# One ring of four PSUM banks instead of two rings of two, from the state space stage on, in a two-block network kernel

## The chip, the cores and the metric

The kernel runs on 1 core of one Trainium2 chip, one launch from inputs to output. The time is the device time of that core in microseconds (us). All arithmetic of the reference is in float32. Where the text says median, it is the median over separate executions; the profile is of one further execution.

## The reference, cut to what matters

The reference is two blocks, `x = first_block(...)` and then `second_block(x, ...)`, on 256 tokens of width 1024. The first block (attention with an index, latent attention, cross attention, mixture of experts) is not touched. The second has two layers, and a second stream of 256 context tokens (`ctx`) beside `x`:

```python
def second_block(x, c, ctx, ...):
    for i in range(2):
        h_lat, h_ctx = modulated rmsnorm of x and of ctx
        if i == 0:  o_ctx, o_lat = ssd_mixer(h_ctx, h_lat, ...)     # state space, 8 groups of 4 heads
        else:       o_ctx, o_lat = attn_mixer(h_ctx, h_lat, ...)
        x = x + g1l * o_lat
        x = x + g2l * moe_ec(...)                                   # 16 experts choose their tokens
        if i == 0:  ctx = ctx + g1c * o_ctx;  ctx = ctx + g2c * moe_ec(...)
    return rmsnorm(x, final_norm_w)

# inside ssd_mixer, per group and chunk of 128 tokens:
    seg    = exp(where(tri, acum[..., :, None] - acum[..., None, :], -inf))
    cb     = einsum('bclgn,bcsgn->bcgls', Cc, Bc)
    y_diag = einsum('bcgrls,bcsgrp->bclgrp', cb[:, :, :, None] * seg, xdt)
    y_off  = einsum('bclgn,bcgrpn,bcgrl->bclgrp', Cc, h_prev, exp(acum))
    out    = rmsnorm((y + D_skip * x) * silu(z), norm_w) @ out_w
```

## The kernel before

The program is written against a tile framework. Tiles are taken from pools; a pool's tag with `bufs=n` is a ring of n buffers, and the framework makes the (n+1)th tile of a tag wait until the first has been read for the last time. The framework's scheduler then sets the order of each engine's instructions from the program order and its own model of when buffers come free (`schedule_with_timeline_sim=True` at the end of the listing). So a change of a ring's size changes the order in which instructions stand on the engines, and each engine then works its list strictly in that order. DMAs to and from DRAM are nearly all issued by SyncE (SP), in such a list too.

PSUM has 8 banks of 128 x 512 floats. `ps(tag)` (L93 to L95) takes one bank from a tag's ring; `psum(**bufs)` (L98) opens a set of rings. `run` (L2078) opens the set `four` (L2083) once for everything from the state space stage up to the end of layer 0's experts, and again for layer 1's experts. Between them the attention stage has its own set (`L=1, M=1, t=2, b=2`). The four tags of `four`:

- "p" (2 banks): projections (L1302 to L1304, `mm3`, three matmuls for each product of split floats), the modulation vectors (L1235), half of `ssd_out`, an expert's accumulators.
- "y" (2 banks): the outputs of a group (`yps`, L1576), the other half of `ssd_out`, accumulators.
- "t" (2 banks): the transposes (L1280, L1532, L1537, and in the experts' part L1721, L1750, L1761, L1842, L1861), and the product of the states with C (L1599), which DVE reads at L1600.
- "b" (2 banks): all other small products: `cb` (L1552), `seg` (L1563 and L1566), state sums (L1588), decays (L1594), the norm (L1656), the routing products (L1764, L1785), and the products that put the experts' outputs back in the tokens' places (L1873).

**State space stage** (about 438 to 1020 us). First the normed rows are transposed (`to_features_mod`, L1280): PE transposes, DVE scales into z (L1286), ACT rounds (L1287), POOL subtracts (L1288). Then 8 groups: `ssd_project` makes six projections of a group, each 24 matmuls of 128x512 into one "p" bank (weights through the ring "wr" of two, loaded at L1476 and L1478, split by ACT and DVE at L1296 and L1297); `ssd_group` does the rest. A group has four steps (two halves q, two s-tiles). A step forms three `seg` tiles: PE at L1563 (and L1566 for two of them) into a "b" bank, ACT's exponential at L1568 into one of three SBUF buffers "seg"; POOL adds the second to the first (L1570), DVE multiplies by `cb` into M (L1573, two buffers), and PE multiplies M with the transposed x (L1576, 8 matmuls). A group takes 5 "t" tiles and 18 "b" tiles in all, and ends with a store of y (L1615) by SP. The scheduler lays a group's work between the projections of the next group; group 7 has no next group. After it comes `ssd_out` (L1617), first for ctx, then for x: its weights go through a ring of three (L1634) and two split buffers; of each group's two halves one goes into "p" banks and one into "y" banks.

**Experts, layer 0** (about 1047 to 1517 us): 4096-byte rows of expert weights stream from DRAM (L1668), PE multiplies at L1824, and after each second product the output is put back (L1873): for two halves n and four token tiles, two matmuls into a "b" bank, read by DVE at L1876. **Attention, layer 1** (about 1505 to 1692), then **experts, layer 1** (about 1714 to 2155) and the last norm.

Of the kernel before, what the change touches and what calls it, by code (L numbers as in the profile page):

```python
# [79 lines left out]
class Net:  # L80
# [11 lines left out]

    def ps(self, tag, n=512, dt=F32):  # L93
        self.n += 1
        return self.pp.tile([P, n], dt, tag=tag, name=f"ps{self.n}", bufs=self.pb[tag])  # L95

    @contextmanager
# [200 lines left out]
    def lin(self, ps, w, hT, i, ks):  # L298
        for j, k in enumerate(ks):
            self.nc.tensor.matmul(ps, lhsT=hT[:, k, i * P:(i + 1) * P], rhs=w[:, j, :],  # L300
                                  start=(j == 0), stop=(j == len(ks) - 1))
# [1506 lines left out]
    def choice_group(self, l, grp, EG, S, samples, xg, aff, pos, gr, actT, whole, tile_):  # L1808
# [5 lines left out]
        def product(nm, x, nk=4):  # L1814

            tag = self.turn("py")
            ps = [self.ps(tag) for _ in range(2)]
            ne = 4 // nk
            for q in range(8 // nk):
                ws = [self.choice_tile(nm, l, e0 + j, nk, q) for j in range(0, EG, ne)]  # L1820
                for k in range(nk * q, nk * q + nk):
                    for n, p in enumerate(ps):
                        for j in range(EG):
                            nc.tensor.matmul(p[j * S:(j + 1) * S], lhsT=x(k, j),  # L1824
                                             rhs=ws[j // ne][:, j % ne, k % nk, n * 512:(n + 1) * 512],
                                             start=(k == 0), stop=(k == 7), tile_position=(0, j * S))
            return ps
# [250 lines left out]
    def run(self):  # L2078
        self.small = "f"
        self.first()  # L2080
        self.small = "b"
        nc = self.nc
        four = dict(p=2, y=2, b=2, t=2)  # L2083
        with ExitStack() as right, self.psum(**four):
            out_, _ = self.ssd(right)
            ap = self.ctx.enter_context(self.pool("attt"))
            with self.pool("ch0") as pool, self.weight_slots(2), ExitStack() as more:
                o = self.choice(0, [(self.ctx_x, 1), (self.x, 0)], pool)
                with self.pool("chs0") as tp:
                    tmp_ = self.cut(tp)  # L2090
                    self.ssd_out(0, out_)
                    self.choice_route(o, 0, tmp_)
                    self.ssd_out(1, out_)
                    self.attention_tables(ap)
                    right.close()
                    more.enter_context(self.weight_slots(5, "right"))
                    self.choice_route(o, 1, tmp_)
                self.hold = [self.ctx_x[:, 1, 1023:]] * 2
                with self.pool("chf0") as fp:
                    self.choice_run(o, self.cut(fp))  # L2100
                self.hold = None
        with ExitStack() as slots, ExitStack() as right, ExitStack() as ps:
            A = slots.enter_context(self.weight_slots(3))
            ps.enter_context(self.psum(L=1, M=1, t=2, b=2))
            with self.pool("att") as ap:
                oT, ao = self.attention(ap, right)
            pool = slots.enter_context(self.pool("ch1"))
            o = self.choice(1, [(self.x, 0)], pool)
            B = slots.enter_context(self.weight_slots(2))
            self.slots = A * 3  # L2110
            self.attention_out(oT, ao)
            right.close()
            ps.close()
            C = slots.enter_context(self.weight_slots(4, "right"))
            self.slots, self.slot = A * 3 + B * 2 + C * 4, 0
            with self.psum(**four):
                with self.pool("chs1") as tp:
                    self.choice_route(o, 0, self.cut(tp), self.ctx_x)
                with self.pool("chf1") as fp:
                    self.choice_run(o, self.cut(fp), self.ctx_x)  # L2120
                src, g = self.a["final_norm_w_2"], self.ctx_x[:, 0]
                nc.sync.dma_start(g, bass.AP(tensor=src.tensor, offset=src.offset, ap=[[0, P], [1, D]]))
                self.finish(g)
# [32 lines left out]
```

## Time and profile before

| what | us |
|---|---|
| median of 3 runs | 2175.62 (2175.52 to 2177.86) |
| the profiled execution, its own time | 2176.17 |
| its span in the trace | 2174.4 |
| PE busy, share of the span | 1884.1 (87%) |
| DVE busy | 981.1 (45%) |
| ACT busy | 642.5 (30%) |
| POOL busy | 448.0 (21%) |

Busy time is the sum of an engine's instructions in the trace. Matmuls overlap in the array, so a busy PE need not be at its peak. The granted clock of PE is given as a share of its full 2.4 GHz; 0.5 is 1.2 GHz. What ended a wait is written behind an instruction in brackets as [idle before it <- the instruction that released it].

### The profile page before, as it was taken

Reading aid. Unit: us, or ns where it says so; the run is one execution under the profiler, and the core shown is the slowest. Engines: PE = TensorE matmul, PEld = TensorE weight load, DVE = VectorE, ACT = ScalarE, POOL = GpSimd, SP = SyncE. Lnnn points to the kernel's source line nnn. Section 1 sums busy time; section 2 is a strip of 40 time slices with the busy share of each in tenths; the row PEclk is TensorE's granted clock in tenths of the full one; section 3 lists DMA queues with packets and bytes.
Section 4 is the critical chain, followed back from the end, with each engine's and each line's share of the span. In section 5 each row is a group of like instructions: output and inputs, shape, how many; then the busy total and the mean of one; then the engine's idle time right before and its main releaser. Section 6 shows DMA issues by size and latency. Waiting matters only on the chain. (4 is left out here: it accounts for less than half of the span.)

```text
span 2174.4 us, 23593 instructions
## 1 busy us (share of the span) xinstructions
PE 1884.1 (87%) x9008; PEld 1023.7 (47%) x9008; DVE 981.1 (45%) x1675; ACT 642.5 (30%) x1210; POOL 448.0 (21%) x479
## 2 busy tenths in 40 slices
PE   7989879989999999889899999997989777767666
PEld 6767644356767776567333333333655321111111
DVE  6786542269777777658322222222666411010101
ACT  6554421264444555435100000002444200000000
POOL 4340110033323333511011111111753000000000
PEclk9999979989999999999899999999899899899988
DMA  7554839843322222274899999997537899999996
GB/s 232 190 207 155 309 139 384 340 141 103 117 89 85 90 90 71 88 267 160 353 427 428 426 427 427 427 427 305 204 126 282 326 428 427 427 427 427 427 425 269
DMA packets 128565, 603.49 MB, mean 278 GB/s; under 512 B 18123, under 2 KB 58734, under 8 KB 87998
## 3 DMA queue, kind: packets, MB, share of 16 engines
q1 hardware_dynamic: 128446, 601.92, 69.9%
q8 instruction: 73, 1.20, 0.2%
q14 instruction: 46, 0.38, 0.1%
HBM read 597.10 MB, written 4.78 MB: 277 GB/s over the span
## 5 line engine op out<-in xcount | busy, mean ns | idle before, releaser
L1824 PE MATMUL ps<-w,xg 128*64 128x512 f32 (+1 forms) x2048 | 462.9, 641 | 93.4 <-DMA w<-in_moe_w_dram 93.4
L1824 PEld LDWEIGHTS ps<-w,xg 128*64 128x64 f32 (+1 forms) x2048 | 134.1, 127 | 380.9 <-issue 243.7
L1877 POOL TENSOR_TENSOR x<-x,o 128x512 f32<-128x512 f32 x24 | 38.8, 1618 | 667.8 <-DVE o L1876 667.8
L1302 PE MATMUL ps<-hT,ws 128*128 128x512 f32 x384 | 156.1, 406 | 5.0 <-DVE ada L1237 4.5
L1303 PE MATMUL ps<-hT,ws 128*128 128x512 f32 x384 | 156.1, 406 | 0.0
L1304 PE MATMUL ps<-hT,ws 128*128 128x512 f32 x384 | 154.6, 403 | 0.0
L1824 PE MATMUL ps<-w,ctx 128*32 128x512 f32 x512 | 108.4, 659 | 36.8 <-DMA w<-in_moe_w_dram 35.8
L1867 DVE SCALAR_TENSOR_TENSOR y<-ps,s,y 128x512 fp32r<-128x512 f32 x24 | 17.9, 747 | 248.7 <-ACT y L1866 248.7
L1824 PE MATMUL ps<-w,actT 128*64 128x512 f32 x512 | 124.4, 596 | 3.4 <-ACT actT L1862 1.9
L1508 DVE SCALAR_TENSOR_TENSOR conv<-pad,cols,conv 128x512 f32<-128x512 f32 x124 | 112.0, 904 | 2.6 <-ACT conv L1501 0.4
L1866 ACT ACTIVATE y<-ps,s 128x512 fp32r<-128x512 f32 x24 | 16.5, 686 | 316.8 <-PE ps L1824 260.4
L1302 PEld LDWEIGHTS ps<-hT,ws 128*128 128x128 f32 x384 | 73.0, 190 | 25.2 <-DVE ada L1237 5.2
L1876 DVE TENSOR_TENSOR o<-ps,g 128x512 f32<-128x512 f32 x80 | 52.3, 687 | 65.9 <-PE ps L1873 62.4
L1297 DVE TENSOR_TENSOR ws<-wr,ws 128x1024 fp32r<-128x1024 f32 x48 | 62.3, 1298 | 43.0 <-ACT ws L1296 36.6
L1303 PEld LDWEIGHTS ps<-hT,ws 128*128 128x128 f32 x384 | 73.1, 190 | 18.0 <-issue 3.8
L1304 PEld LDWEIGHTS ps<-hT,ws 128*128 128x128 f32 x384 | 73.0, 190 | 16.9 <-issue 1.9
L1824 PEld LDWEIGHTS ps<-w,ctx 128*32 128x32 f32 x512 | 25.7, 115 | 114.2 <-DMA w<-in_moe_w_dram 58.2
L1824 PEld LDWEIGHTS ps<-w,actT 128*64 128x64 f32 x512 | 42.9, 136 | 73.8 <-issue 66.2
L1297 DVE TENSOR_TENSOR ws<-w,ws 128x1024 fp32r<-128x1024 f32 x46 | 65.3, 1422 | 23.9 <-ACT ws L1296 23.6
L1570 POOL TENSOR_TENSOR seg<-seg,seg 128x512 f32<-128x512 f32 x32 | 47.1, 1471 | 115.7 <-ACT seg L1568 101.0
L1568 ACT ACTIVATE seg<-ps 128x512 f32<-128x512 f32 x96 | 54.8, 597 | 51.0 <-PE ps L1566 28.4
L1573 DVE TENSOR_TENSOR M<-seg,cb 128x512 f32<-128x512 f32 x64 | 54.8, 871 | 30.3 <-ACT seg L1568 20.3
(643 smaller groups left out, 3636.9 us busy)
## 6 DMA issues: line engine op xcount, KB each, us to landing
w<-in_moe_w_dram SPq DMA_DIRECT2D x164, 2048.0 KB
w<-in_moe_w_dram SPq DMA_DIRECT2D x56, 1024.0 KB
v<-in_ada_w_dram SPq DMA_DIRECT2D x16, 1024.0 KB
w<-in_moe_w_up_dram SPq DMA_DIRECT2D x16, 1024.0 KB
w<-in_moe_w_gate_dram SPq DMA_DIRECT2D x16, 1024.0 KB
w<-in_moe_w_down_dram SPq DMA_DIRECT2D x16, 1024.0 KB
wr<-in_ssd_in_w_dram SPq DMA_DIRECT2D x16, 1024.0 KB
w<-in_ssd_out_w_dram SPq DMA_DIRECT2D x32, 512.0 KB
```

Of the source, the lines that this page charges most:

```text
L1297: (eng or self.nc.vector).tensor_tensor(lo, x, hi.bitcast(F32), op=OP.subtract)
L1302: t.matmul(p, lhsT=L[0], rhs=R[0], start=start, stop=False, **kw)
L1303: t.matmul(p, lhsT=L[0], rhs=R[1], start=False, stop=False, **kw)
L1304: t.matmul(p, lhsT=L[1], rhs=R[0], start=False, stop=stop, **kw)
L1508: nc.vector.scalar_tensor_tensor(seq(cv), pad[:, :, j:j + 256], tap(j), seq(cv), op0=OP.mult, op1=OP.add)
L1568: nc.scalar.activation(e, p, AF.Exp)
L1570: nc.gpsimd.tensor_tensor(ex[0][0], ex[0][0], ex[1][0], op=OP.add)
L1573: nc.vector.tensor_tensor(M[:, :, s], e, cb[:, st, None, s].to_broadcast([P, 4, P]), op=OP.mult)
L1824: nc.tensor.matmul(p[j * S:(j + 1) * S], lhsT=x(k, j), rhs=ws[j // ne][:, j % ne, k % nk, n * 512:(n + 1) * 512], start=(k == 0), stop=(k ...
L1867: nc.vector.scalar_tensor_tensor(y[:, 1], p, ws, y[:, 0].bitcast(F32), op0=OP.mult, op1=OP.subtract)
L1876: nc.vector.tensor_tensor(o, q, gr[s][:, c], op=OP.mult)
L1877: (nc.gpsimd if i else nc.vector).tensor_tensor(xx[:, i, c], xx[:, i, c], o, op=OP.add)
```

## The change

```diff
     def ps(self, tag, n=512, dt=F32):
         self.n += 1
+        tag = tag if tag in self.pb else "b"
         return self.pp.tile([P, n], dt, tag=tag, name=f"ps{self.n}", bufs=self.pb[tag])
...
-        four = dict(p=2, y=2, b=2, t=2)
+        four = dict(p=2, y=2, b=4)
```

Where `four` is open, a tile asked for under "t" now comes from "b", which has four banks. The number of banks stays at eight, and each computation is as before. The first block and the attention stage keep their sets. In the changed program every line after L94 is one higher. A group of the state space stage now takes 23 tiles in turn from one ring of four.

The scheduler's order changes with it. Three places follow, all on PE.

The first is the end of the state space projections. Before, the matmuls of the last projection (`ps2074`, L1302 to L1304) stand among group 6's steps (`ps2009` is group 6's second cb, `ps2012` to `ps2023` its seg tiles):

```order
L1302 MATMUL ps2074_9786<-hT0_1281_6200,ws0_2072_9782 128x512
L1303 MATMUL ps2074_9786<-hT1_1282_6201,ws0_2072_9782 128x512
L1304 MATMUL ps2074_9786<-hT0_1281_6200,ws1_2073_9783 128x512
L1552 MATMUL ps2009_9458<-xbc_1970_9304,xbc_1964_9262 128x256 x2
L1563 MATMUL ps2012_9464<-RR0_1351_6453,LBg_1987_9399 128x512
L1566 LDWEIGHTS identb_1331_6367
L1566 MATMUL ps2012_9464<-maskb_1332_6369,identb_1331_6367 128x512
L1576 MATMUL ps1991_9407<-M_2002_9436,xtm_1982_9381 64x256 x2
L1576 MATMUL ps1992_9408<-M_2002_9436,xtm_1982_9381 64x256 x2
L1563 MATMUL ps2014_9469<-RR1_1369_6511,LBg_1989_9403 128x512
```

Now group 6 stands wholly ahead of the last projection, which is followed by group 7's btm, cb and seg tiles (`ps2081`, `ps2088`, `ps2091` to `ps2102`):

```order
L1304 MATMUL ps2074_9786<-hT1_1282_6201,ws0_2072_9782 128x512
L1305 MATMUL ps2074_9786<-hT0_1281_6200,ws1_2073_9783 128x512
L1538 MATMUL ps2081_9833<-const_75,xbc_2057_9686 128x128 x2
L1553 MATMUL ps2088_9847<-xbc_2063_9728,xbc_2057_9686 128x256 x2
L1564 MATMUL ps2091_9853<-RR0_1351_6453,LBg_2082_9837 128x512
L1567 LDWEIGHTS identb_1331_6367
L1567 MATMUL ps2091_9853<-maskb_1332_6369,identb_1331_6367 128x512
L1564 MATMUL ps2093_9858<-RR1_1369_6511,LBg_2084_9841 128x512
```

So two and a half steps of group 6 have moved from behind the last projection to before it, with group 7's x transposes; two steps' seg products of group 7 stand in a row, ahead of its first product with M.

The second place is the start of the stage, the transposes of x (four "t" tiles, `ps1311` to `ps1320`). Before, two tiles are worked off and the third and fourth follow one at a time, the last behind the first projection matmuls (`wdt`):

```order
L1280 MATMUL ps1317_6316<-const_75,xbc_1303_6267 128x128
L1302 MATMUL ps1334_6375<-hT0_1281_6200,wdt0_1326_6357 64x512
L1303 MATMUL ps1334_6375<-hT1_1282_6201,wdt0_1326_6357 64x512
L1304 MATMUL ps1334_6375<-hT0_1281_6200,wdt1_1327_6358 64x512
L1302 MATMUL ps1334_6375<-hT0_1281_6200,wdt0_1326_6357 64x512
L1280 MATMUL ps1320_6329<-const_75,xbc_1301_6265 128x128
L1280 MATMUL ps1320_6329<-const_75,xbc_1303_6267 128x128
```

Now all four are begun at once and done before the first projection matmul:

```order
L1281 MATMUL ps1311_6290<-const_75,xbc_1300_6264 128x128
L1281 MATMUL ps1314_6303<-const_75,xbc_1300_6264 128x128
L1281 MATMUL ps1317_6316<-const_75,xbc_1301_6265 128x128
L1281 MATMUL ps1320_6329<-const_75,xbc_1301_6265 128x128
L1236 MATMUL ps1346_6437<-adaw_1345_6435,silu_c_336 32x512 x4
L1281 MATMUL ps1311_6290<-const_75,xbc_1302_6266 128x128
```

The third is the end of layer 0's experts. Before, the put-back products go two tiles at a time (`ps2737`, `ps2739`, then `ps2741`, `ps2743`):

```order
L1873 MATMUL ps2737_12871<-y_2736_12868,back_2715_12718 128x512
L1873 MATMUL ps2739_12877<-y_2736_12868,back_2715_12718 128x512
L1873 MATMUL ps2737_12871<-y_2736_12868,back_2715_12718 128x512
L1873 MATMUL ps2739_12877<-y_2736_12868,back_2715_12718 128x512
L1873 MATMUL ps2741_12883<-y_2736_12868,back_2715_12718 128x512 x2
```

Now all four tiles get the first of their two matmuls, and then all four the second:

```order
L1874 MATMUL ps2737_12871<-y_2736_12868,back_2715_12718 128x512
L1874 MATMUL ps2739_12877<-y_2736_12868,back_2715_12718 128x512
L1874 MATMUL ps2741_12883<-y_2736_12868,back_2715_12718 128x512
L1874 MATMUL ps2743_12889<-y_2736_12868,back_2715_12718 128x512
L1874 MATMUL ps2737_12871<-y_2736_12868,back_2715_12718 128x512
L1874 MATMUL ps2739_12877<-y_2736_12868,back_2715_12718 128x512
```

The second half n (`ps2746` to `ps2752`) stands as before. On SP the stores of y (L1615) of a group move ahead of two or three of the weight loads of later groups that they stood behind.

## Rows read from the trace of the kernel before

**Rows 1.** The profile's page: busy us, share of the span, instructions of each engine
```profile
PE 1884.1 (87%) x9008; PEld 1023.7 (47%) x9008; DVE 981.1 (45%) x1675; ACT 642.5 (30%) x1210; POOL 448.0 (21%) x479
```

**Rows 2.** The page: the chain that ended last, by line
```profile
DMA w<-in_moe_w_dram 16%; PE ps L1824 4%; PE ps L2046 1%; PE ps L2028 1%; PE ps L1785 0%; PE ps L1235 0%; PE ps L1302 0%; PE ps L1304 0%; PE ps L1303 0%; PE ps L2011 0%; PE ps L2012 0%; ACT ws L1296 0%; ACT L L2020 0%; DVE x L2075 0%; DVE o L1876 0%
```

**Rows 3.** Windows: from:to, length, busy PE, PEld, DVE, ACT, POOL; clock, DMA share, GB/s
```profile
510.00:850.00 340.00, 334.71 (x1573) 245.51 (x1573) 261.84 (x316) 169.64 (x278) 99.26 (x133) 0.99 0.28 86
...
1050.00:1500.00 450.00, 421.30 (x1735) 158.82 (x1733) 108.90 (x213) 39.24 (x73) 50.05 (x36) 1.00 0.99 418
1750.00:2150.00 400.00, 282.16 (x1383) 71.59 (x1378) 30.73 (x57) 13.47 (x26) 9.67 (x6) 0.90 1.01 426
```

**Rows 4.** Windows of the end of the state space groups
```profile
864.87:883.14 18.27, 16.37 (x73) 10.23 (x72) 14.32 (x17) 9.62 (x17) 10.88 (x12) 0.91 0.59 184
883.14:911.65 28.51, 21.84 (x95) 12.46 (x94) 15.13 (x18) 13.45 (x24) 14.54 (x14) 0.88 0.14 51
```

**Rows 5.** Timeline of PE, same stretch: start, us, line, operation, [idle before <- releaser]
```profile
864.41 0.40 PE L1303 MATMUL ps<-hT,ws 128*128 128x512 f32 x1
864.64 0.39 PE L1304 MATMUL ps<-hT,ws 128*128 128x512 f32 x1
...
871.38 0.50 PE L1563 MATMUL ps<-RR,LBg 128*128 128x512 f32 x1 [1.44 <-ACT seg L1568]
...
897.01 1.98 PE L1576 MATMUL ps<-M,xtm 128*64 128x256 f32 x8
...
905.31 0.50 PE L1563 MATMUL ps<-RR,LBg 128*128 128x512 f32 x1 [1.43 <-ACT seg L1568]
905.75 1.08 PE L1576 MATMUL ps<-M,xtm 128*64 128x256 f32 x8
...
911.65 0.58 PE L1302 MATMUL ps<-ws,y 128*128 128x512 f32 x1
```

**Rows 6.** Single lines over the whole span: durations in ns, min/median/max
```profile
L1568 ACT ACTIVATE seg<-ps x96: 575/597/622, 519.2 to 905.9; 128x512 f32<-128x512 f32 x96
...
L1570 POOL TENSOR_TENSOR seg<-seg,seg x32: 1261/1338/2262, 526.4 to 905.8; 128x512 f32<-128x512 f32 x32
...
L1573 DVE TENSOR_TENSOR M<-seg,cb x64: 676/691/1762, 528.3 to 907.6; 128x512 f32<-128x512 f32 x64
```

**Rows 7.** Timeline of POOL at the start of the state space stage
```profile
456.73 1.43 POOL L1288 TENSOR_TENSOR hT<-z,hT 128x256 fp32r<-128x256 f32 x2 [0.98 <-ACT hT L1287]
458.66 1.44 POOL L1288 TENSOR_TENSOR hT<-z,hT 128x256 fp32r<-128x256 f32 x2 [0.51 <-ACT hT L1287]
```

**Rows 8.** Timeline of PE at the end of layer 0's experts
```profile
1507.72 1.33 PE L1873 MATMUL ps<-y,back 128*128 128x512 f32 x4 [0.62 <-DVE o L1876]
1510.24 1.03 PE L1873 MATMUL ps<-y,back 128*128 128x512 f32 x2 [1.19 <-ACT y L1866]
1512.02 1.22 PE L1873 MATMUL ps<-y,back 128*128 128x512 f32 x2 [0.76 <-DVE y L1867]
1513.60 2.08 PE L1873 MATMUL ps<-y,back 128*128 128x512 f32 x4 [0.36 <-DVE o L1876]
```

**Rows 9.** Timelines of PE (L1599) and DVE (its reader, L1600)
```profile
570.35 0.59 PE L1599 MATMUL ps<-xbc,hs 128*128 128x256 f32 x2
...
572.60 0.67 DVE L1600 TENSOR_TENSOR eF<-eF,ps 128x512 f32<-128x512 f32 x1
```

**Rows 10.** Timeline of SP's queue: y stores of a group, then the next weight load
```profile
750.43 3.51 SPq L1615 DMA_DIRECT2D yd<-xbc  x2
764.18 0.38 SPq L1478 DMA_DIRECT2D wr<-in_ssd_in_w_dram  x1
```

**Rows 11.** Waits of SP's queue, 840 to 1550: total us, times, longest
```profile
SPq L1668 <- PE ps L1824: 400.7, 84, 20.8
```

**Rows 12.** Windows in ssd_out for ctx
```profile
940.00:950.00 10.00, 7.24 (x31) 5.34 (x29) 3.84 (x4) 2.37 (x4) 0.00 (x0) 1.00 0.99 384
950.00:960.00 10.00, 6.21 (x17) 4.52 (x18) 2.45 (x2) 2.94 (x3) 0.00 (x0) 0.66 0.84 309
```

## The prediction

> **What bounds the kernel now.** I read the page first: PE is busy 87% of the span and no other engine reaches half [rows 1]. The chain that ended last is made of expert weights from DRAM and of PE [rows 2]. Since an average over stages hides which of the two ends last where, the windows by stage come next [rows 3]. In the projections of the state space stage PE is busy 334.71 of 340.00 us at a clock of 0.99 with DMA at 0.28 of its time: PE alone sets the pace there. In both expert stages the reader should see the opposite, 418 and 426 GB/s at a DMA share of 0.99 and 1.01: their length is the length of the weight stream, and PE's waits inside them cost nothing.
>
> A change to PSUM rings can then shorten only places where PE or DMA is not full. I looked for those in the stages that use the changed set. The largest is the end of the state space groups, between the last projection matmul, which starts at 864.64, and the first matmul of ssd_out's second half at 911.65 [rows 5]. There no projections are left to fill PE while ACT, POOL and DVE work on a group. The windows [rows 4] give the loss: idle time is 18.27 - 16.37 = 1.90 us in the first part (the rest of group 6) and 28.51 - 21.84 = 6.67 in the second (group 7). The granted clock falls to 0.91 and 0.88 of 2.4 GHz; matmuls stretched that way count as busy, so (1 - 0.91) x 18.27 = 1.64 and (1 - 0.88) x 28.51 = 3.42 us more. In the timeline the same 8 matmuls of L1576 take 1.98 us at 897.01 and 1.08 at 905.75 [rows 5]: half clock after the idle stretch against full clock. The loss is 3.54 + 10.09 = 13.6 us. The two longest waits, 1.44 and 1.43 us, are all on ACT's exponential of a seg tile [rows 5]: the third seg product of a step waits for one of the two "b" banks.
>
> **The change part by part.** The sum is made against the profiled execution, 2176.17 us, which lies 0.55 above the median of 2175.62.
>
> *End of the groups.* In the changed order group 6 stands ahead of the last projection's end, where PE has no idle time to lose, and only group 7 is left behind it. That takes away the first part's 3.5 us in whole, and two steps' seg products in a row take away waits of the second. What cannot go is group 7's own chain. A step needs two exponentials before the POOL sum and one DVE product before its first seg buffer is free again: 2 x 0.597 + 1.338 + 0.691 = 3.22 us by the medians [rows 6], so four steps 12.9 us, plus some 1.1 for the last product with M and an entry of about 2 (an estimate: cb and the first seg products at the paces of rows 5). That is 16 us. PE's own work there is the 46.78 us of rows 4 less the loss, 33.2, less what moves ahead: of the first part's 18.27 - 3.54 = 14.7 us some 12 are group 6's, the other 12 matmuls are ssd_out's at 0.23 us each (864.64 - 864.41), and 1 us of transposes: 20 us. Chain and work are then about equal, and two things that take turns never overlap in full. I keep 3.5 us, a quarter of the old loss, as the estimate. Gain 13.6 - 3.5 = **10.1 us**; bounds 3.5 (only group 6's part goes) and 13.6.
>
> *Start of the stage.* Four transposed tiles at once instead of two. POOL, the last in that chain, waits 0.98 and 0.51 us for ACT [rows 7]. Faster transposes cannot give more than these 1.5; I take **1.0 us**, bounds 0 and 1.5.
>
> *End of layer 0's experts.* Behind the last weights the put-back products wait 0.62, 1.19, 0.76 and 0.36 us [rows 8]. The two on DVE's o (0.62 and 0.36) are ring waits, the other two wait for y itself, and DVE remains to read eight tiles. I take **1.0 us**, bounds 0 and 2.9. Earlier, inside the stream, the same edit is worth nothing, covered by the DMA share of 0.99 [rows 3].
>
> *Inside the projections.* Only 340.00 - 334.71 = 5.3 us is idle there [rows 3]; the new order neither adds nor removes matmuls, so I put 0, bounds 2 of gain and 4 of loss, and treat a larger loss as a rival.
>
> *SP.* Two y stores wait 3.51 us in SP's queue at 750.43; the next weight load is issued at 764.18 only because its buffer comes free then [rows 10]. So a store that moves ahead of a load has 764.18 - 753.94 = 10.2 us of cover. Cost 0; if that cover is gone, the wait falls on the next projection.
>
> *Does the gain reach the end?* Layer 0's weight loads wait 84 times, 400.7 us in all, for PE's L1824 to free their buffers [rows 11]: the stream follows PE, so an earlier start of PE is an earlier end. Attention and layer 1's experts have the same instructions in nearly the same order and move as a block.
>
> *Rule against row.* The row shows PE with 5.3 us to spare in the projections. The Trainium skill, page Perfetto Trace Analysis, section Identifying the Most-Contended Engine, says matmul busy time is a bad measure of headroom and that the busy share of weight loads should be read instead. That measure is the base of the last rival; by it alone there would be hidden room where I put 0.
>
> Sum: 2176.2 - 10.1 - 1.0 - 1.0 = 2164.1 for a profiled execution, 2163.5 for a median.
>
> **The rivals.**
>
> 1. *Only group 6's part goes.* Group 7's loop stays bound by three seg buffers, POOL and DVE, so PE idles and its clock falls as before. For it: L1570 took up to 2.262 us and L1573 up to 1.762 [rows 6], and SBUF buffers are unchanged. Against: the waits seen were for banks. Gain 3.5 + 1.0 + 0.5 = 5.0, time 2170.6.
>
> 2. *A wait between groups (slower).* With 23 tiles a group in one ring of four, the next group's transposes and cb take the banks of the previous group's last four tiles, which include L1599's two. DVE reads the last one 572.60 + 0.67 - 570.35 = 2.9 us after PE began it, because convolutions stand before it in DVE's queue [rows 9]; transposes used to wait only for transposes. PE is in order, so a bank read late stops the projections behind it too. It decides once this wait exceeds the projections placed in between. A whole group has 48 matmuls of one half x 0.23 = 11 us of cover against 2.9 seen; at 7 group borders, 1.7 us each would eat the 12.1 us gained. At 3 us each the price is 21, the time 2163.5 + 21 = 2184.5.
>
> 3. *The gain is swallowed before the stream (no change).* ssd_out is short of weights at 940 to 960: PE is busy 13.45 of 20 us, DMA at 0.99 and 0.84 [rows 12]. If that transfer does not move with PE, only the two small terms stay: 2176.2 - 2.0, by the median 2173.6. Against: SP issues these loads in order behind loads whose buffers PE frees.
>
> 4. *Hidden room in the projections.* Weight loads are busy 245.51 of 340.00 us, 72% [rows 3]. If what keeps PE from loading without a break were ring waits that the matmuls' overlapping records hide, at most 340.0 - 245.5 = 94.5 us could go; I take half, 47: 2163.5 - 47 = 2116.5. Against: small products have other shapes, and the trace shows no wait. This is where the page's rule, named above, would lead.
>
> **How the numbers follow.** Forecast 0.58, rival 1 0.17, rival 2 0.12, rival 3 0.10, rival 4 0.03. The forecast's own bounds run from 2176.2 - 18.0 - 2 - 0.55, about 2155.6, up to 2176.2 - 3.5 + 4 - 0.55, about 2176. I give **2163.5 us**, range **2155 to 2176**: it holds the forecast, rival 1 and rival 3 and leaves out rival 2, rival 4 and some 0.05 of tails. A measurement of this kernel can tell 0.2%, 4.35 us, from no change. Rival 4 and the forecast are faster by more, and of rival 1, at 5.0, two thirds: 0.58 + 0.03 + 0.11 = 0.72. Rival 3 and the rest of rival 1 are the same: 0.16. Slower is rival 2: 0.12.
>
> **What would show it.** Right: in the profile after, the time from the last projection matmul to the first one of ssd_out's second half shrinks from 47 us to about 24, the clock in it stays above 0.95, L1564's waits for ACT's seg fall, the projections' windows stay at 98% busy, and choice 0's first saturated window comes some 11 us sooner. Wrong: PE waits at L1533, L1538 or L1553 for DVE's eF or ACT inside the projections (rival 2); clock and idle time in group 7's part as before (rival 1); an unchanged start of the expert stream (rival 3). The prediction falls if the projections lose PE share.

## The result, and the profile after

The changed kernel took 2160.68 us (median of 4 runs, 2159.34 to 2164.36) beside 2176.74 for the kernel before: ratio 0.9923, 95% interval 0.9911 to 0.9936. A second set of runs (experiment 4 below) gave 2163.79 beside 2174.91, ratio 0.9947 (0.9934 to 0.9961). So the change is worth 11 to 17 us by the two sets, which barely agree; ratios from different sets that lie within 0.0024 of each other are not told apart here. Forecast were 2163.5 us and a gain of 12.1. The profiled execution took 2164.36 us, 11.8 less than the profiled one of before.

The page after, busy time by engine (from here on, every line number of the changed program is one higher than before):

```profile
PE 1868.7 (86%) x8993; PEld 1026.0 (47%) x9008; DVE 985.1 (46%) x1675; ACT 642.7 (30%) x1210; POOL 449.8 (21%) x479
```

That is little against [rows 1]; what happened is seen only by stage. The windows after, first the middle of the projections as in [rows 3], then the projections (first to last projection matmul) and the end of the groups (last projection matmul to the first of ssd_out's second half):

```profile
510.00:850.00 340.00, 330.84 (x1549) 243.15 (x1563) 265.13 (x317) 175.29 (x290) 116.42 (x142) 0.98 0.28 87
459.30:882.34 423.04, 408.97 (x1902) 300.81 (x1913) 329.32 (x423) 215.31 (x348) 144.99 (x175) 0.98 0.28 87
882.34:904.63 22.29, 20.99 (x103) 13.21 (x103) 16.11 (x19) 14.37 (x25) 13.75 (x14) 1.00 0.52 168
```

The same two stretches in the kernel before:

```profile
462.50:864.64 402.14, 392.79 (x1838) 288.20 (x1834) 315.63 (x409) 205.65 (x331) 124.81 (x160) 0.99 0.29 90
864.64:911.65 47.01, 38.45 (x168) 22.88 (x167) 29.68 (x34) 23.07 (x40) 25.41 (x26) 0.89 0.31 102
```

Take lost time as in the prediction, idle plus (1 - clock) x length (the clock has two digits, so the second part is good to 2 us in 400, and a difference of two such figures to 4). The end of the groups fell from 8.6 + 5.2 = 13.7 lost to 1.3, at full clock. But the projections rose from 9.4 + 4.0 = 13.4 lost to 14.1 + 8.5 = 22.5. Of some 12 us won at the end, 9 or more were given back in the stage where the prediction saw no cost. Over the whole stage, from its first transposition to ssd_out's second half, lost time hardly moved, though the stage is 6.6 us shorter. The same windows, before and after:

```profile
438.54:911.65 473.11, 447.32 (x2079) 319.83 (x2078) 360.65 (x476) 241.80 (x400) 165.22 (x208) 0.97 0.31 96
438.12:904.63 466.51, 441.34 (x2066) 319.39 (x2080) 361.45 (x476) 242.75 (x402) 172.22 (x208) 0.97 0.31 96
```

PE idles 25.8 us in one and 25.2 in the other, at a clock of 0.97 in both (good to 2 us of lost time). What fell is its busy time, by 6.0 us for the same computations. The modulation products (L1235, later L1236) account for 3.4 of these: over these windows they keep PE busy for 17.95 us before and 14.53 after. Before, four of them stand in two parts with other matmuls in between, and the two halves of one take 1.05 us each (at 692.56 and 695.50 below), while a whole one takes 1.06. What the other 2.6 us come from was not followed.

The end of the groups in the timeline of PE after, against [rows 5]:

```profile
882.34 0.39 PE L1305 MATMUL ps<-hT,ws 128*128 128x512 f32 x1
...
888.07 0.50 PE L1564 MATMUL ps<-RR,LBg 128*128 128x512 f32 x1 [0.97 <-ACT seg L1569]
...
889.22 1.08 PE L1577 MATMUL ps<-M,xtm 128*64 128x256 f32 x8
...
904.63 0.58 PE L1303 MATMUL ps<-ws,y 128*128 128x512 f32 x1
```

Of seven waits for ACT's exponential in this stretch (six at seg products, one at cb) one of 0.97 us is left, and the first eight matmuls of L1577 take 1.08 us at once. Part of the cover is ssd_out's: before, its 24 matmuls of this stretch stand ahead of group 7's steps (874.71 to 886.1); now they stand between them (890.57 to 900.8). The loss inside the projections is in the table of waits of PE between 459.26 and 904.61 (total us, times, longest):

```profile
PE ps L1303 <- DVE ada L1238: 9.2, 5, 1.8
PE ps L1244 <- DVE ada L1238: 3.1, 2, 1.8
PE ps L1236 <- DMA adaw<-in_ada_w_dram: 1.1, 1, 1.1
```

Once in each group from 600 us on, PE waits 1.83 us for DVE's addition of a modulation product (ada, L1238). In five groups a projection (L1303) waits, and what it waits for is a bank. In the sixth L1244 waits, which transposes the sum itself: that wait is for data, whatever the bank. Before, PE waited twice for ada, 4.5 us. One of the five places, PE first, then DVE and ACT:

```profile
705.10 1.06 PE L1236 MATMUL ps<-adaw,silu_c 128*32 128x512 f32 x8
706.09 1.09 PE L1533 MATMUL ps<-const,xbc 128*128 128x128 f32 x8
709.01 0.50 PE L1303 MATMUL ps<-hT,ws 128*128 128x512 f32 x1 [1.83 <-DVE ada L1238]
...
709.60 0.63 PE L1305 MATMUL ps<-hT,ws 128*128 128x512 f32 x1
...
705.93 1.76 DVE L1606 TENSOR_TENSOR xbc<-xbc,z 128x512 f32<-128x512 f32 x1
707.62 0.74 DVE L1509 SCALAR_TENSOR_TENSOR conv<-pad,cols,conv 128x512 f32<-128x512 f32 x1
708.28 0.67 DVE L1238 TENSOR_TENSOR ada<-ada,ps 128x512 f32<-128x512 f32 x1
...
704.90 0.63 ACT L1609 ACTIVATE z<-xbc 128x512 f32<-128x512 f32 x1 [4.50 <-DVE xbc L1606]
...
707.61 0.77 ACT L1502 ACTIVATE conv<-ps,cols,cols 128x512 f32<-128x512 f32 x1
```

The modulation product sits in one of the two banks of ring "p", and the projection ahead of it in the other. In the changed order the old group's matmuls are finished by then, only the next group's transposes stand behind the product, and the z projection comes next. DVE is still at the old group's last multiplications and a convolution and reads the product at 708.28; the projection starts 0.06 us after DVE is through. So it was given the product's own bank: this framework does not hand out a ring's banks strictly in turn, which would have given it the other one. But the other one was late too. ACT, which had waited 4.50 us for the old group's DVE work, reads it (L1502 last) until 708.38, only 0.6 us earlier. Both readers of ring "p" stand behind the old group's end. In the kernel before, the same place looks like this, PE, then ACT and DVE:

```profile
692.56 1.05 PE L1235 MATMUL ps<-adaw,silu_c 128*32 128x512 f32 x4
...
695.50 1.05 PE L1235 MATMUL ps<-adaw,silu_c 128*32 128x512 f32 x4
696.48 0.50 PE L1302 MATMUL ps<-hT,ws 128*128 128x512 f32 x1
...
693.88 0.77 ACT L1501 ACTIVATE conv<-ps,cols,cols 128x512 f32<-128x512 f32 x1
...
699.67 0.67 DVE L1237 TENSOR_TENSOR ada<-ada,ps 128x512 f32<-128x512 f32 x1
```

Nothing stands between the end of the product and the projection, DVE reads the product 3 us later, and there is no wait: ACT had read the other bank by 694.65. In the change, the wait has a tail: at 709.60 a matmul takes 0.63 in place of 0.39 us, the clock having been granted at its lower level soon after the idle time.

### The profile page after: what moved, and what is told of

It reads as the page before. It is cut to its first block, busy times and chain, and to the rows that moved or that the text cites. A ratio compares the mean times of both kernels' runs of the same rounds, so it can differ in the third digit from the quotient of the medians.

```text
span 2162.4 us, 23552 instructions
## 1 busy us (share of the span) xinstructions
PE 1868.7 (86%) x8993; PEld 1026.0 (47%) x9008; DVE 985.1 (46%) x1675; ACT 642.7 (30%) x1210; POOL 449.8 (21%) x479
## 5 line engine op out<-in xcount | busy, mean ns | idle before, releaser
L1303 PE MATMUL ps<-hT,ws 128*128 128x512 f32 x384 | 158.2, 412 | 9.8 <-DVE ada L1238 9.2
L1304 PE MATMUL ps<-hT,ws 128*128 128x512 f32 x384 | 155.6, 405 | 0.0
L1509 DVE SCALAR_TENSOR_TENSOR conv<-pad,cols,conv 128x512 f32<-128x512 f32 x124 | 104.2, 841 | 2.0
L1303 PEld LDWEIGHTS ps<-hT,ws 128*128 128x128 f32 x384 | 74.5, 194 | 31.7 <-DVE ada L1238 10.3
L1304 PEld LDWEIGHTS ps<-hT,ws 128*128 128x128 f32 x384 | 74.3, 194 | 18.0 <-issue 3.1
L1574 DVE TENSOR_TENSOR M<-seg,cb 128x512 f32<-128x512 f32 x64 | 63.1, 1002 | 33.9 <-ACT seg L1569 21.8
L1877 DVE TENSOR_TENSOR o<-ps,g 128x512 f32<-128x512 f32 x80 | 52.3, 686 | 56.1 <-PE ps L1874 52.2
L1298 DVE TENSOR_TENSOR ws<-wr,ws 128x1024 fp32r<-128x1024 f32 x48 | 61.5, 1281 | 22.9 <-ACT ws L1297 22.8
L1297 ACT ACTIVATE ws<-w 128x1024 fp32r<-128x1024 f32 x52 | 54.4, 1056 | 49.4 <-PE ps L1305 31.8
```

The lines of the kernel that those rows point to most:

```text
L1297: self.nc.scalar.activation(hi, x, AF.Copy)
L1298: (eng or self.nc.vector).tensor_tensor(lo, x, hi.bitcast(F32), op=OP.subtract)
L1303: t.matmul(p, lhsT=L[0], rhs=R[0], start=start, stop=False, **kw)
L1304: t.matmul(p, lhsT=L[0], rhs=R[1], start=False, stop=False, **kw)
L1509: nc.vector.scalar_tensor_tensor(seq(cv), pad[:, :, j:j + 256], tap(j), seq(cv), op0=OP.mult, op1=OP.add)
L1574: nc.vector.tensor_tensor(M[:, :, s], e, cb[:, st, None, s].to_broadcast([P, 4, P]), op=OP.mult)
```

## The experiments

Every kernel was timed beside the kernel before in five rounds. The table has, by each kernel's one profile, length / lost time of the two stretches, and the whole stage from its first transposition to ssd_out's second half.

| kernel | ratio (95%) | projections | end of groups | stage |
|---|---|---|---|---|
| before | 1 | 402.1 / 13.4 | 47.0 / 13.7 | 473.1 |
| the change | 0.9923 (0.9911 to 0.9936) | 423.0 / 22.5 | 22.3 / 1.3 | 466.5 |
| 1: change, ada in b | 0.9824 (0.9810 to 0.9837) | 402.7 / 0.3 | 22.8 / 0.9 | 441.6 |
| 2: change, p 3, b 3 | 0.9871 (0.9856 to 0.9885) | 402.4 / 1.4 | 26.1 / 3.6 | 452.3 |
| 3: change, ada behind z | 0.9871 (0.9857 to 0.9885) | 406.5 / 11.5 | 27.0 / 4.9 | 454.7 |
| 4: the change again | 0.9947 (0.9934 to 0.9961) | 423.4 / 22.5 | 22.1 / 1.3 | 466.5 |
| 5: before, ada in b | 0.9961 (0.9949 to 0.9973) | 397.3 / 4.8 | 52.2 / 14.8 | 465.2 |
| 6: before, b 3, t 1 | 0.9914 (0.9899 to 0.9930) | 411.4 / 6.9 | 23.8 / 2.1 | 455.7 |
| 7: before, b 3, t 1, ada in b | 0.9908 (0.9893 to 0.9923) | 411.0 / 6.1 | 26.8 / 6.2 | 455.6 |
| 8: p 3, b 3, ada in b | 0.9894 (0.9879 to 0.9909) | 390.0 / 0 | 46.9 / 10.7 | 451.9 |
| 9: four banks in the state space stage only | 0.9945 (0.9932 to 0.9957) | as the change | as the change | 466.6 |
| 10: four banks for the experts only | 0.9990 (0.9979 to 1.0002) | 402.4 / 13.4 | 46.7 / 13.6 | 473.4 |

A stretch's length alone says little, since the scheduler puts different work into it; lost time and above all the stage as a whole can be compared.

**1. Is it the bank in ring p?** The changed kernel, the modulation products from b:

```diff
-            self.ada_tile, self.ada_ps = lambda: self._t(pp, [P, 2 * D], "adaw", 1), "p"
+            self.ada_tile, self.ada_ps = lambda: self._t(pp, [P, 2 * D], "adaw", 1), "b"
```

> The changed kernel with one more edit: the modulation products of the state space stage (L1236, read by DVE at L1238) take their bank from the ring b in place of p. Theory: in the changed kernel the z projection of each group waits 1.83 us for DVE to read the modulation product's bank in ring p (five times L1303, once L1244), with half clock behind some of these waits; this is what ate part of the gain inside the projections. Without it the waits of PE on DVE ada fall from 12.3 us to under 2, the stretch from 510 to the last projection is some 9 us shorter, and the time is 7 to 11 us below the changed kernel's: 2150 to 2154, ratio 0.988 to 0.990 to the kernel before. Rival: DVE is late for whatever comes there, so the wait moves to the next product that needs DVE or to the ring b; then the time stays within 3 us of the changed kernel's, ratio 0.991 to 0.994.

Measured 2140.51 us. The direction was that of the theory, the size was not: the stage fell by 25 us against the change. The windows of the same two stretches:

```profile
456.35:859.02 402.67, 402.35 (x1921) 296.22 (x1932) 331.30 (x428) 215.53 (x350) 139.29 (x177) 1.00 0.30 94
859.02:881.86 22.84, 21.98 (x115) 14.71 (x114) 15.63 (x19) 15.41 (x27) 14.39 (x16) 1.00 0.59 205
```

PE is idle for 0.3 us in 402.7, at full clock. Over the whole stage idle time fell from 25.2 to 10.8 us and the clock rose from 0.97 to 0.99, so lost time explains nearly all of the 25. The 12.3 us of named waits were a little over half of the price: lost time fell by 22.2, since other idle time and the lower clock behind the waits went too. And DVE is no earlier than before; PE first, then DVE, at one of these products:

```profile
695.07 1.07 PE L1236 MATMUL ps<-adaw,silu_c 128*32 128x512 f32 x8
696.07 0.50 PE L1303 MATMUL ps<-hT,ws 128*128 128x512 f32 x1
...
696.58 1.76 DVE L1298 TENSOR_TENSOR ws<-wr,ws 128x1024 fp32r<-128x1024 f32 x1
698.26 0.68 DVE L1238 TENSOR_TENSOR ada<-ada,ps 128x512 f32<-128x512 f32 x1
```

DVE adds the product 2.1 us after PE is done with it (695.07 + 1.07 to 698.26), as late as in the changed kernel (705.10 + 1.06 to 708.28), but the projection stands right behind it and starts at once. The rival, that DVE's lateness would move the wait elsewhere, fell. This is the fastest version of the study.

**2. The same from the other side:** ada stays in p, p gets a third bank.

```diff
-        four = dict(p=2, y=2, b=4)
+        four = dict(p=3, y=2, b=3)
```

> The changed kernel with one bank moved from the shared ring to the projections: p 3, y 2, b 3 (transpositions in b, modulation products in p). Theory: a third bank in p takes away the wait for the modulation bank, while three shared banks still hold a step's three seg tiles; waits on DVE ada under 3 us, loss at the end of the groups 2 to 6 us, ratio 0.983 to 0.989. Rival: with transpositions in three shared banks the groups fall behind the projections again (loss at the end of the groups 8 us or more), ratio 0.990 to 0.996.

2150.08 us, as the theory had it. The timeline of PE, then DVE:

```profile
792.99 1.06 PE L1236 MATMUL ps<-adaw,silu_c 128*32 128x512 f32 x8
793.98 0.50 PE L1303 MATMUL ps<-hT,ws 128*128 128x512 f32 x1
...
795.20 0.68 DVE L1238 TENSOR_TENSOR ada<-ada,ps 128x512 f32<-128x512 f32 x1
```

Modulation product, then at once the projection, though DVE reads the product only at 795.20. With the first run this shows that the projection's wait was for a bank of ring p, and that neither a projection right behind the product nor DVE's lateness costs anything by itself.

**3. The same by the order:** rings as in the change, the modulation step written behind the two z projections.

```diff
-        self.ada_step(2 if g == 0 else 1)
         xs, BT, CT = out[:2], out[2], out[3]
...
             zz.append(z)
+        self.ada_step(2 if g == 0 else 1)
         return xs, BT, CT, zz
```

> The changed kernel, rings as in the change (modulation products in p), but each group's modulation step is written behind its two z projections in place of ahead of them. Theory: the 1.83 us waits come from the bank of ring p that the modulation product holds while DVE works off a group's end, right ahead of the next projection; with other work behind the product on PE (cb and seg products stand there in the order) the waits on DVE ada fall below 4 us and the time comes 6 to 18 us below the changed kernel's: 2143 to 2155, ratio 0.984 to 0.990. Rival: DVE's lateness at that point is the cause, whatever the order; the wait stays, ratio 0.991 to 0.994.

2151.64 us, as the theory had it; no wait of PE on ada is left. What still is lost in the projections is mostly one wait of 6.38 us at the stage's start, of L1447 for DVE's scol, a price of this order.

**4. The change again,** for a second profile, with no edit.

> The changed kernel as it is, once more, for a second profile and an interval. The first profile's execution took 2164.36 us, the median of its runs was 2160.68. Theory: the stretches up to the end of the state space stage repeat within 0.5 us (last projection matmul 423 us behind the first, six waits of 1.83 us on DVE ada), and what differs between executions lies in the expert stages, which follow DRAM; ratio 0.991 to 0.9935. Rival: the waits inside the projections were a chance of that execution; then they are gone or smaller here and the projections' stretch is under 415 us.

The projections' lost time is the same, with the same six waits of 1.83 us. The rival, chance, is out. The ratio, 0.9947, lies above the theory's range, and its interval just touches it. The profiled execution took 2161.52 us against 2164.36: of those 2.8 us, 1.8 lie behind the first expert matmul (1039.9 and 1039.0 us), 0.5 ahead of the stage.

**5. Do the two edits add?** The kernel before with the first experiment's edit.

> The kernel before (two pairs) with the modulation products of the state space stage taken from the ring b in place of p. Theory: in the kernel before the modulation bank in ring p cost little, 4.5 us of waits on DVE ada, since group work stood behind the product; so this edit alone gives 0 to 6 us, ratio 0.997 to 1.000, and the gain that it gave on top of the change, 20 us, exists only because the change's order put the next projection right behind the modulation product. Rival: the wait on ring p costs the same before, hidden in other rows; then this kernel gains 12 to 20 us by itself, ratio 0.991 to 0.9945, and the two edits simply add.

2169.79 us, 8.6 less than before: a little more than the theory's 0 to 6, far less than the 20 to 23 us that the same edit gives on top of the change. The end of the groups is as bad as ever:

```profile
455.52:852.84 397.32, 392.53 (x1832) 288.27 (x1850) 296.62 (x399) 206.04 (x331) 125.96 (x165) 1.00 0.29 91
852.84:905.01 52.17, 41.01 (x190) 24.28 (x191) 34.64 (x49) 26.34 (x46) 26.90 (x29) 0.93 0.35 118
```

So the edits don't add. With pairs, the loss at the end stays (11.2 idle + 3.7); with four banks and ada in p, the loss at the end becomes a loss in the middle; of these four kernels only the one with both edits is rid of both.

**6 and 7. Is it the pooling, or the third bank?** The kernel before with the eight banks dealt otherwise; then with ada in b as well.

```diff
-        four = dict(p=2, y=2, b=2, t=2)
+        four = dict(p=2, y=2, b=3, t=1)
```

> The kernel before with the eight banks dealt otherwise: three for b, one for t, in place of two and two. Theory: what the end of the groups lacks is a third bank for the third seg product of a step; with three the waits of PE's seg products on ACT's exponential fall and the loss between the last projection and ssd_out's second half falls from 13.6 to 6 or less, while one bank for transpositions costs 1 to 4 us where they come in pairs (the stage's start, the x transposes): time 2168 to 2174, ratio 0.996 to 0.999. Rival: the gain is due to the pooling, that is to group 6's work moving ahead of the last projection, which needs more than three: loss as before, and with the transpositions' cost the ratio is 1.000 to 1.003.

> Three banks for b, one for t, two for p and two for y, and the modulation products from b. Theory: pooling is not what matters; a third bank for the seg products and a free ring p are, so this comes within 6 us of the changed kernel with modulation products in b (2140.5): ratio 0.981 to 0.986. Rival: with the modulation products among the three b banks, steps wait for banks again and only part is left: ratio 0.986 to 0.992.

Without ada in b: 2159.72 us, level with the change. A third bank for a step's third seg tile takes the loss at the end from 13.7 to 2.1 us; pooling is not needed for that. But here too the scheduler has moved group 6's steps ahead of the last projection, so the run doesn't part the bank's own effect from that of the move. I had put the cost of a single bank for transposing too high and had not foreseen that the modulation products would fare better here. PE, then ACT and DVE, in run 6:

```profile
703.47 1.06 PE L1235 MATMUL ps<-adaw,silu_c 128*32 128x512 f32 x8
705.25 0.59 PE L1302 MATMUL ps<-hT,ws 128*128 128x512 f32 x1
...
704.35 0.77 ACT L1501 ACTIVATE conv<-ps,cols,cols 128x512 f32<-128x512 f32 x1
...
705.39 0.68 DVE L1237 TENSOR_TENSOR ada<-ada,ps 128x512 f32<-128x512 f32 x1
```

Only four matmuls of L1599 stand behind the product, less than the eight transposes of the change. The projection starts before DVE has read the product, 0.13 us after ACT is through with the other bank (705.12). With ada in b: 2159.38, no better. The theory (within 6 us of 2140.5) fell, the rival's range held: as soon as three b banks carry ada too, 6 us are lost at the end again.

**8. Is there more to win in ring p?** Run 2's banks with ada in b.

> Three banks for p, two for y, three shared ones, and the modulation products from the shared ones. Theory: with four shared banks and the modulation products in b PE had no idle time left in the projections (402.35 of 402.67 us busy), so a third bank for p can add nothing there, and three shared banks cost 1 to 4 us at the end of the groups: time 2141 to 2147, ratio 0.983 to 0.986. Rival: the start of the stage and ssd_out gain from the third p bank: below 2139, ratio under 0.982.

2151.11 us, in neither range. PE is busy for all of the projections (390.03 of 390.03 us), which are shorter because the scheduler now leaves group 6's work behind them again: the end is 46.9 us long with 8.8 idle. So PE's share in the projections alone is no measure of the stage.

**9 and 10. Which stage?** Four banks up to the routes and pairs from layer 0's experts on; and the converse. The set of banks is closed and opened anew between them:

```diff
+                banks.close()
+                banks.enter_context(self.psum(p=2, y=2, b=2, t=2))
                 self.hold = [self.ctx_x[:, 1, 1023:]] * 2
```

> Four shared banks only up to the end of the state space stage and of the routes; from layer 0's experts on the two pairs again. Theory: the state space stage gives some 7.5 of the change's gain (the first expert product came 7.5 us earlier) and the expert stages and their ends the rest, so this kernel gains 7 to 10 us: ratio 0.9955 to 0.9968, and the stretch from the last expert product of layer 0 to attention's first score product is 80 to 81 us as before. Rival: the gain behind the experts is not from their banks (another order of attention, or chance); then the ratio is that of the change, 0.992 to 0.9935.

> The converse: two pairs in the state space stage, four shared banks only in the expert stages of both layers. Theory: 3 to 6 us of gain, from the end of layer 0's experts and attention's start, ratio 0.9972 to 0.9986; the end of the state space groups stays at 47 us with a loss of 13 to 14. Rival: no change, 0.9990 to 1.0010, all of the gain is the state space stage's.

2166.41 and 2174.65 us: 0.55% of gain from the state space stage's banks, and none that can be told from zero from the experts' alone. The first ratio, 0.9945, lies between the theory's range (0.9955 to 0.9968) and the rival's (0.992 to 0.9935), and its interval touches both; the second, 0.9990, lies at the edge of the rival's range, and its interval reaches into the theory's. How the gain behind the state space stage divides is therefore left open; 0.9945 is also what the change itself gave in experiment 4 (0.9947). Both kernels carry a cost of the reopening that is not separated: the first expert matmul comes 35.4 and 35.6 us behind ssd_out's last, 25.8 in the change, of which all but 2.6 and 4.2 us are made up by the end of layer 0's experts. The small term at that end is confirmed. PE's timeline in the change, against [rows 8]:

```profile
1496.92 2.11 PE L1874 MATMUL ps<-y,back 128*128 128x512 f32 x8
1499.81 0.73 PE L1874 MATMUL ps<-y,back 128*128 128x512 f32 x2 [0.78 <-ACT y L1867]
1501.05 1.93 PE L1874 MATMUL ps<-y,back 128*128 128x512 f32 x6 [0.51 <-DVE y L1868]
```

and with pairs for the experts (run 9):

```profile
1498.86 1.52 PE L1874 MATMUL ps<-y,back 128*128 128x512 f32 x4
1500.99 1.33 PE L1874 MATMUL ps<-y,back 128*128 128x512 f32 x4 [0.62 <-DVE o L1877]
```

The two waits on DVE's o are gone with four banks, those on y stay. From the last expert matmul to attention's first transposition it takes 14.8 us before, 14.9 in run 9, 13.9 in the change and in run 10.

## Why the prediction was right, point by point

It was right in time and sign, and in what happens at its largest term, the end of the groups. That the sum came within 1 us of the profiled gain is luck: of the 11.8 us, 7.5 were won ahead of the experts, where 11.1 had been forecast, and 3.4 in attention, where nothing had. And of the 7.5 hardly any is lost time; most is busy time that the prediction took as fixed. By its own last sentence ("falls if the projections lose PE share") it failed inside the projections.

- *End of the groups, forecast -10.1.* Right, sized small: lost time fell by 12.4. The 3.5 us kept for group 7's own chain were 1.3; two steps' seg products in a row and ssd_out's 24 matmuls between the steps cover it, in what parts is not shown. The forecast of 24 us for the stretch, with a clock above 0.95, stands beside 22.3 at 1.00.
- *Inside the projections, 0, at worst 4.* This is the step that failed: lost time rose by 9, and the share of PE from 510 to 850 fell from 334.71 to 330.84 us of 340. The prediction counted the matmuls, which did not change, and took the trace's small idle time as the bound. It did not ask when the readers of ring p, which the diff doesn't touch, get to its banks in the new order: ACT and DVE are still at the old group's end when the next projection is due. Runs 1, 2 and 3 remove the wait in three ways. It is not that work is missing behind the product: in the kernel before (696.48) and in run 6 (705.25) as little stands there, without a wait. Why the framework gave the projection the product's own bank stays open.
- *Start of the stage, -1.0.* Not shown. The stretch up to the first projection fell from 24.0 to 21.2 us, past the bound of 1.5, but 12 of its 22 matmuls of `wdt` now stand behind it, 12 x 0.23 = 2.8 us of work, which is all of the difference. With three shared banks (run 2) all 22 stand there, and it takes 23.9.
- *End of layer 0's experts, -1.0.* 14.8 to 13.9 us: right.
- *SP, 0.* Right: no wait of PE for projection weights arose, only 1.1 us for early modulation weights, against 3.0 before. (The 3.51 us of [rows 10] that the prediction calls a wait is the length of the row from the first store to the end of the second.)
- *Passing 1:1.* Right. ssd_out's last matmul came 7.6 us earlier (1021.7 to 1014.2) and the first expert matmul 7.5 (1047.4 to 1039.9; the sign that the prediction named was some 11); SP's loads still wait on PE:

```profile
SPq L1669 <- PE ps L1825: 402.2, 78, 21.7
```

- *Attention, "moves as a block".* Not quite: from its last transposition to its first score product it took 46.5 us after, in both profiles of the change, against 49.9 before and 50.1 in run 5. Before, PE waits there once; PE, then DVE:

```profile
1570.57 1.75 PE L1928 MATMUL ps<-const,kr 128*128 128x128 f32 x7 [3.82 <-DVE kB L1984]
...
1566.33 1.47 DVE L1237 TENSOR_TENSOR ada<-ada,ps 128x512 f32<-128x512 f32 x2
1567.72 2.20 DVE L1979 TENSOR_TENSOR kr<-a,rowv 128x512 f32<-128x512 f32 x2
1569.84 1.27 DVE L1984 TENSOR_TENSOR kB<-ps,kA 64x512 fp32r<-64x512 f32 x2
```

  Two modulation additions stand ahead of kr and kB in DVE's list. After, kr comes first, and no wait is left there. That is a by-product of the scheduler's order, worth 3.4 us, more than a third of what the projections lost. Runs 9 and 10 have it both (46.2 and 44.6 us), so it needs neither set of banks in particular.

Of the rivals, the first (group 7 as before) is out by the 1.3 us left, the third (swallowed before the stream) by the expert matmuls' 7.5 us. The second was right in kind, a bank read late that stops the projections, and wrong in place: no wait of PE at the transposes or at cb for the old group's readers is in the trace, and the wait was in ring p. The fourth (hidden room in the projections) is out. In run 1 PE is busy 402.35 of 402.67 us with weight loads at 296.22, 74%; in the kernel before the share was 72% [rows 3]. So with PE never idle weight loads are busy three quarters of the time, and the missing quarter was no room that any run here reached. The Trainium skill's page Perfetto Trace Analysis, section Identifying the Most-Contended Engine, would have headroom judged by that share and by the matmul work done against the peak. Here the share alone told nothing of what could be won, 2 points for all of the lost time, though the share of matmul time alone hid the low clock.

## What to carry to other kernels

When a ring is made larger and a scheduler reorders, ask of every other ring in the stage how late the readers of all its banks will be in the new order, and which bank the next tile is given; work that moves forward can put its own end ahead of those readers. Price such a wait by what PE loses in all, idle time and lower clock together: here six waits of 1.83 us and some smaller ones stood for 22 us. Judge a stage by its length and lost time from end to end, since a saturated middle can just mean that the work was left for the end (run 8), and look at busy time too: another order can make the same matmuls shorter.

## What the runs showed of the hardware

Right behind the first five waits of 1.83 us the granted clock of the changed kernel was 0.66, 1.00, 0.66, 0.66 and 1.00 of 2.4 GHz in 5 us (from 602.5, 656.5, 709, 763 and 817 us), so partly at the lower level of 1.2 GHz behind three of them. In the second profile of the same program (experiment 4) it was 0.66, 0.66, 1.00, 0.66 and 0.66: the waits are the same, but others of them are followed by the lower level. The first two of the first profile, and the second of the second:

```profile
602.50:607.50 5.00, 4.99 (x15) 3.96 (x16) 4.96 (x5) 2.00 (x4) 4.23 (x3) 0.66 0.97 311
656.50:661.50 5.00, 4.92 (x22) 4.08 (x23) 4.96 (x6) 2.06 (x4) 4.26 (x3) 1.00 0.97 299
...
655.90:660.90 5.00, 4.98 (x15) 3.95 (x16) 4.96 (x5) 2.01 (x4) 4.24 (x3) 0.66 0.98 300
```

What decides that was not tried.

The four matmuls of a modulation product, each on 32 columns of its own, are eight records in the trace. Together they take 1.06 us (705.10 in the changed kernel); two of them, four records, take 1.05 alone (692.56 in the kernel before). So a product that stands in two parts costs about as much as two products.
